# Tile 1's attention: the context rows' norm in nine steps, context projections in four parts, a modulation of three operations

## The chip, the core and the metric

The kernel runs on one core of a Trainium2 chip. The core has five engines that work side by side, each with its own instruction queue: TensorE (PE, matrix products; PEld are its weight loads), VectorE (DVE), ScalarE (ACT), GpSimd (POOL) and SyncE (SP), which here only issues DMA transfers. GpSimd's queue carries DMA issues too. An engine takes its instructions in order and waits on semaphores for what another engine or a DMA has to have done.

The metric is the device time of one execution in microseconds (us). The kernel before took 1836.33 us, the median of 3 runs (1835.45 to 1843.21).

## What is computed

A backbone of two layers over 1024 latent rows and 256 context rows of width 1024. Layer 0 is windowed attention with 16 heads of 64 (4 key-value heads, so 4 query heads to each), layer 1 a bidirectional state-space mixer (SSD). Ahead of each layer the rows are normed and modulated, behind it they are added through a gate:

```python
for i in range(DEPTH):
    shift, scale, gate = adaln(c, w_ada[i], b_ada[i])
    shift_c, scale_c, gate_c = adaln(c_ctx, w_ada[i], b_ada[i])
    u = rms_normalize(h) * (1.0 + scale[:, None]) + shift[:, None]
    uc = rms_normalize(hc) * (1.0 + scale_c) + shift_c
    ...
        y, yc = attention_mixer(u, uc, ...)   # layer 0
        y, yc = ssd_mixer(u, uc, ...)         # layer 1
    h = h + gate[:, None] * y
    if need_ctx_out:
        hc = hc + gate_c * yc
return rms_normalize(h) * final_norm_w
```

In the attention a block of 128 queries sees the key blocks beside it (up to 3) and the 2 blocks of context keys; context queries see only the context. The result is multiplied by silu(g) and goes through w_out, the output projection.

## The kernel before

The rows lie as columns: a row tile holds 128 features by n rows, and a full set of rows is 8 such pieces (k or m from 0 to 7). There are three row tiles: i = 0 and i = 1 are 512 latent rows each, i = 2 the 256 context rows. For accuracy every product of a projection is made of three: each operand is split into a high and a low part in float32r (uH and uL for the rows, wh and wl for the weights), and `mm3` (lines 236 to 238) multiplies high by high, high by low and low by high. A weight half is loaded by SP (line 229, into wr), cast on ScalarE (wh, line 222) and the rest taken off on GpSimd in this stage (wl, line 224).

Rows are normed by `rstd_c` (two small matmuls, line 367 with line 369's copy to sbuf as its end) and by `modulate` (line 290), which for one piece multiplies h by the row factor r (line 297, VectorE), applies scale and shift (line 298, ScalarE), casts to uH (line 299, ScalarE) and subtracts for uL (line 300, VectorE). It is called 40 times: for tile 1's and the context's rows of layer 0 by the first norm, and for all three tiles of layer 1.

The attention (`attention`, line 695) goes over units of one query block and one key-value head, 8 context units, then 16 of tile 0, then 16 of tile 1. `att_front` loads a unit's queries (qs and qz on GpSimd's DMA queue, sgt on SP's), makes the four heads' scores (lines 645 and 646), and the softmax (line 649 on VectorE, 651 on ScalarE). `att_back` then goes over the key blocks: four transposes (line 670), a cast to ph on ScalarE (674), a subtraction to pl on VectorE (675), and two matmuls with the values (676 and 677). qz holds one head's queries with zeros in the other half; the zeros are written once, by the memset of line 711, on VectorE.

After each key block `tick` advances the filler, so that TensorE has projections to do while the softmax runs. The filler is a list of generators; one call of `advance` runs one of them up to its next yield, a part. `tick` spreads the parts evenly: by the time of key block s of the stage's count, total x s / count parts are done. `self.tc.high_priority` and `issue_after` around them say where the scheduler may place the part: behind a matmul of the attention a few blocks back.

In tile 1's attention the filler is `out_steps(2)`, the context rows' output projections, and then `out_steps(0)`, tile 0's. `one(m)` makes one of 8 pieces of the output: it loads and splits the weights, loads the residual into the ring of two slots named h1 (SP), multiplies in PARTS = 8 parts (each one contraction step, three matmuls of n columns), adds through the gate (line 736, VectorE), stores h to DRAM (SP), squares it (ScalarE) and adds the squares up (line 744, GpSimd). `fin` norms the tile for layer 1: `rstd_c`, then for each of the 8 pieces a load of h from DRAM into the same ring of two (line 756) and `modulate`, all in one part. So the order of the filler's parts is: 64 for the context, 1 for its norm, 64 for tile 0, 1 for its norm: 130, which is what `total[1]` says. Its tile 1 counterpart, `out_steps(1)`, runs after the attention.

Line numbers are those of the kernel before.

Of the kernel before, what the change touches and what calls it, by code (L numbers as in the profile page):

```python
# [9 lines left out]
F32 = mybir.dt.float32  # L10
BF16 = mybir.dt.bfloat16
F32R = mybir.dt.float32r
AF = mybir.ActivationFunctionType
ALU = mybir.AluOpType
# [3 lines left out]
P = 128  # L18
D = 1024
KT = D // P  # L20
# [9 lines left out]
HD = 64  # L30
# [12 lines left out]
    pj=1, S=2, pt=2, pv=1,  # L43
# [5 lines left out]
AHEAD = 1  # L49
PACE = 4  # L50
PARTS = 8
SLACK = (0, 0, 0)
QC = 5
FIRST = 5
# [50 lines left out]
class Kernel:  # L105
# [13 lines left out]
    def t(self, pool, shape, dt, tag, bufs=None):  # L119
        self.n += 1  # L120
        kw = {"bufs": bufs or BUFS.get(tag, 1)}
        return pool.tile(shape, dt, tag=tag, name=f"{tag}_{self.n}", **kw)
# [167 lines left out]
    def modulate(self, layer, h, r, i, k):  # L290

        nc = self.nc
        c = 0 if i < 2 else 1
        m = self.mod[layer]
        sc, sh = m[:, 8 + k, c : c + 1], m[:, k, c : c + 1]
        uh, ul = self.uH[i][:, k, :], self.uL[i][:, k, :]
        nc.vector.tensor_mul(h, h, r)
        nc.scalar.activation(h, h, AF.Identity, bias=sh, scale=sc)
        nc.scalar.copy(uh, h)
        nc.vector.tensor_sub(ul, h, uh)  # L300


    def xin(self, i):
# [80 lines left out]
    def norm0(self, c0, p, wvp):  # L384
# [80 lines left out]
        for n in (0, 2):  # L465
            self.ada0(n, raws[n], ps)
        modulate(0)
        for x in range(G0 // 2):
            half(0, x)
# [22 lines left out]
        with last():  # L492
            self.load_rope(p, 0, LAT)
            load_nat(2)
            load_x(2)
        modulate(1)
        for x in range(G0):
            half(1, x)
# [196 lines left out]
    def attention(self, c0, ckv):  # L695
        nc, t, a = self.nc, self.t, self.a
        ps = self.psA
        BUFS.update(wr=2, wh=3, wl=3, sqt=2)
        self.wp = self.pool("wo", ctx=c0)
        self.pb = self.pool("back", ctx=c0)  # L700
        self.psm = self.pool("sm", ctx=c0)
        p = self.pool("att", ctx=c0)
        t(p, [P, 384], F32, "pad")
        cq = ExitStack()
        pq = self.pq = self.pool("qp1", ctx=cq)
        BUFS.update(qf=2, rope_b=1, qh=1, ql=1)
        self.load_rope(pq, 512, 512)
        oH, oL = [None] * 3, [None] * 3
        self.qz = [t(p, [P, R, P], F32R, f"qz{z}") for z in range(2)]
        for z in range(2):  # L710
            nc.vector.memset(self.qz[z][(1 - z) * HD : (2 - z) * HD].bitcast(F32), 0.0)

        def qg1(src, out, x):
            w = self.load_halves(a[src][x], nc.gpsimd)
            yield
            pj = []
            yield from self.proj_g(pj, ps, w, self.uH, self.uL, 1, parts=PARTS)
            out(pq, pj[0], x, 1)

        def out_steps(i):  # L720
            s, n = TT[i]
            c = 0 if i < 2 else 1
            st = {}

            def one(m):
                p = self.po
                w = self.load_halves(a["wo"][m], nc.gpsimd)
                yield
                h1 = t(self.o1, [P, n], F32, "h1k") if i == 1 else t(p, [P, n], F32, "h1")
                if i == 1:  # L730
                    st[m] = h1
                nc.sync.dma_start(h1, self.xin(i)[m * P : (m + 1) * P, :])
                out = []
                yield from self.proj_g(out, ps, w, oH, oL, i, "S" if i == 1 and m % 3 else "pj", parts=1 if i == 1 else PARTS)
                pj = out[0]
                nc.vector.scalar_tensor_tensor(h1, in0=pj[:, :n], scalar=self.mod[0][:, 16 + m, c : c + 1], in1=h1, op0=ALU.mult, op1=ALU.add)
                nc.sync.dma_start(self.h_d[m][i], h1)
                if m == 0:
                    st["acc"] = t(p, [P, n], F32, "sqa")
                    nc.scalar.activation(st["acc"], h1, AF.Square)  # L740
                else:
                    sq = t(p, [P, n], F32, "ut")
                    nc.scalar.activation(sq, h1, AF.Square)
                    (nc.vector if i == 1 else nc.gpsimd).tensor_tensor(st["acc"], st["acc"], sq, op=ALU.add)

            def fin():
                yield
                p = self.po
                r = self.rstd_c(p, st["acc"], n, D, rout=(p, [P, n], F32, "sqa"), dout=(p, [P, 512], F32, "dg0"))
                self.alloc_u(i)  # L750
                for k in range(KT):
                    if i == 1:
                        h = st[k]
                    else:
                        h = t(p, [P, n], F32, "h1")
                        nc.sync.dma_start(h, self.h_d[k][i])
                    self.modulate(1, h, r, i, k)

            return [lambda m=m: one(m) for m in range(KT)] + [fin]

        pr = [lambda x=x: qg1("wg", self.g_out, x) for x in range(8)] + [lambda x=x: qg1("wq", self.q_out, x) for x in range(8)]
        fill = {2: pr[:QC], 0: pr[QC:], 1: out_steps(2) + out_steps(0)}
        total = {2: QC * PARTS, 0: (16 - QC) * PARTS, 1: 16 * PARTS + 2}
        units = [(i, j, b) for i, blocks in ((2, range(8, 10)), (0, range(0, 4)), (1, range(4, 8))) for b in blocks for j in range(KV)]
        nkb = lambda b: 2 if b >= 8 else 2 + min(b + 2, 8) - max(b - 1, 0)
        count = {i: sum(nkb(u[2]) for u in units if u[0] == i) - SLACK[i] for i in range(3)}
        seen, done = [0, 0, 0], [0, 0, 0]
        self.last = []
        cur = nxt = None

        def tick(flush=False):

            seen[i] += 1
            while done[i] < (total[i] if flush else min(total[i], -(-total[i] * seen[i] // count[i]))):
                advance(i, self.last[max(-len(self.last), -PACE)])

        def advance(i, after):
            nonlocal cur, nxt
            with self.tc.high_priority(offset=-300), self.tc.issue_after(after):
                if cur is None:  # L780
                    cur = nxt or fill[i].pop(0)()
                    if nxt is None:
                        next(cur)
                    nxt = None
                    if fill[i]:
                        nxt = fill[i].pop(0)()
                        next(nxt)
                if next(cur, "end") == "end":
                    cur = None
            done[i] += 1  # L790

        pend = [self.att_front(p, x, *units[x]) for x in range(AHEAD)]
        for _ in range(FIRST):
            advance(2, self.scored.ins)
        for x, (i, j, b) in enumerate(units):
            if oH[i] is None:
                if i == 1:
                    i = 0
                    tick(True)
                    i = 1  # L800
                    cq.close()
                    self.po = self.pool("op", ctx=c0)
                n = TT[i][1]
                oH[i] = t(self.up, [P, KT, n], F32R, f"uH{i}")
                oL[i] = t(self.up, [P, KT, n], F32R, f"uL{i}")
            if x + AHEAD < len(units):
                pend.append(self.att_front(p, x + AHEAD, *units[x + AHEAD]))
            self.att_back(p, pend.pop(0), oH, oL, tick)
        tick(True)
        ckv.close()  # L810
        self.cf = ExitStack()
        self.pf = self.pool("front", ctx=self.cf, side="right")
        self.cdt = ExitStack()
        self.pdt = self.pool("dtp", ctx=self.cdt, side="right")
        with ExitStack() as c1:
            self.o1 = self.pool("o1", ctx=c1, side="right")
            steps = out_steps(1)
            for f in steps[:-1]:
                for _ in f():
                    pass  # L820
            self.dt_setup()
            for i, lo in ((2, 256), (0, 0)):
                n = TT[i][1] // 2
                self.dt_raw(self.dts[:, lo : lo + n], self.proj(ps, self.wdt, i), n)
            for _ in steps[-1]():
                pass
        BUFS.update(wr=2, wh=2, wl=2)
        if "u1" in self.dump:
            for i, (s, n) in enumerate(TT):
                self.dump_split("u1", self.uH[i], self.uL[i], i, n, s)  # L830
# [816 lines left out]
```

## Time and profile before

| what | value |
|---|---|
| median of 3 runs | 1836.33 us |
| the profiled execution, its time | 1840.92 us |
| the profiled execution, its span on the core | 1839.2 us |
| mean granted clock of TensorE | 0.988 of full |
| HBM traffic | 190.88 MB read, 35.13 MB written |

The span is the time from the first to the last instruction that the profiler saw; the time of the execution is a little longer. All times within the span are counted from its start, so "621.13" is a place. Tile 1's attention lies at about 500 to 690 us, the first norm and projections ahead of 100, and layer 1 from some 770 to the end. Busy times of engines overlap each other. Matmuls are pipelined and the rows of neighbours overlap (their ends are modelled); what a matmul costs in a dense stream is the distance between starts. In a row of waits stand the waiting engine with its tile and line, what it waited for, the total in us, how many times, and the longest; in a row of the timeline stand the start, the duration, the instruction, and in brackets the idle time ahead of it and what ended that.

### The profile page before, as it was taken

The page shows a single profiled execution, that of the slowest core. Times are in us where ns is not written, and L with a number is a line of the kernel's source. Part 1 is how long each engine was busy: PE and PEld are TensorE (multiplying, and loading weights), DVE is VectorE, ACT ScalarE, POOL GpSimd, SP SyncE. Part 2 cuts the span into 40 slices and gives each one's busy share as a digit, 9 for nine tenths or more (in the row PEclk, how much of TensorE's full clock was granted, in tenths as well). Part 3 has the DMA queues.
Part 4 walks back from the last instruction along what each step waited for, and adds up shares of the span by engine and source line. Part 5 has one row for each costly group of instructions (what it writes and reads, how often), then busy time and mean ns, then how long its engine had stood idle before and what let it go on. Part 6 is the DMA issues. An engine that isn't in the chain of part 4 may idle for free. (4 is left out here: it accounts for less than half of the span.)

```text
span 1839.2 us, 29059 instructions
## 1 busy us (share of the span) xinstructions
PE 1757.5 (96%) x10319; PEld 1503.1 (82%) x10319; DVE 1171.9 (64%) x2136; ACT 893.0 (49%) x1956; POOL 803.2 (44%) x1066
## 2 busy tenths in 40 slices
PE   6899999999999999899999999999999999999997
PEld 2697778888888787678889898988989898888886
DVE  4544426778887765674766757676675767675643
ACT  3722227777777765562443535344353434454422
POOL 1331116555566454102454554545455454554321
PEclk8999999999999999999999999999999999999998
DMA  8648855544455445321323323232232324456542
GB/s 303 241 127 263 284 179 141 121 97 107 112 130 130 109 129 187 99 70 41 87 69 78 93 66 83 76 92 67 80 93 64 86 73 101 148 165 171 180 138 69
DMA packets 212497, 227.62 MB, mean 124 GB/s; under 512 B 16384, under 2 KB 149632, under 8 KB 212352
## 3 DMA queue, kind: packets, MB, share of 16 engines
q1 hardware_dynamic: 178288, 207.12, 37.8%
q0 software_dynamic: 34064, 18.65, 5.6%
q8 instruction: 81, 1.33, 0.3%
q14 instruction: 64, 0.52, 0.1%
HBM read 190.88 MB, written 35.13 MB: 123 GB/s over the span
## 5 line engine op out<-in xcount | busy, mean ns | idle before, releaser
L236 PE MATMUL pj<-uH,wh 128*128 128x512 f32 (+1 forms) x712 | 256.4, 362 | 11.3 <-ACT uH L457 8.3
L238 PE MATMUL pj<-uH,wl 128*128 128x512 f32 (+1 forms) x712 | 243.7, 343 | 1.2 <-POOL wl L224 1.2
L237 PE MATMUL pj<-uL,wh 128*128 128x512 f32 (+1 forms) x712 | 244.2, 343 | 0.4 <-DVE uL L458 0.4
L1157 POOL TENSOR_TENSOR xw<-xn,dtdec 128x256 f32<-128x256 f32 x144 | 107.6, 750 | 199.5 <-PE psD L1182 127.1
L224 POOL TENSOR_TENSOR wl<-wr,wh 128x512 fp32r<-128x512 f32 x92 | 121.6, 1325 | 117.6 <-ACT wh L222 114.1
L1088 PE MATMUL pj<-uH,wh 128*128 128x512 f32 x512 | 165.9, 400 | 3.6 <-ACT bn L1042 2.2
L236 PEld LDWEIGHTS pj<-uH,wh 128*128 128x128 f32 x712 | 135.8, 191 | 39.2 <-ACT uH L457 9.6
L1088 PE MATMUL pj<-uL,wh 128*128 128x512 f32 x512 | 167.4, 400 | 0.2 <-DVE uL L300 0.2
L1088 PE MATMUL pj<-uH,wl 128*128 128x512 f32 x512 | 166.9, 400 | 0.7 <-DVE wl L1019 0.7
L1113 PE MATMUL pj<-wh,uH 128*128 128x256 f32 x512 | 151.7, 296 | 2.6 <-ACT xn L1042 2.6
L675 DVE TENSOR_TENSOR pl<-pt,ph 128x512 fp32r<-128x512 f32 x168 | 114.5, 687 | 58.2 <-ACT ph L674 57.0
L238 PEld LDWEIGHTS pj<-uH,wl 128*128 128x128 f32 x712 | 135.5, 190 | 18.4 <-POOL wl L224 2.1
L1113 PE MATMUL pj<-wh,uL 128*128 128x256 f32 x512 | 149.8, 293 | 0.0
L237 PEld LDWEIGHTS pj<-uL,wh 128*128 128x128 f32 x712 | 136.0, 191 | 16.9 <-issue 3.1
L1113 PE MATMUL pj<-wl,uH 128*128 128x256 f32 x512 | 147.1, 287 | 0.0
L222 ACT CAST wh<-wr 128x512 fp32r<-128x512 f32 (+1 forms) x132 | 84.7, 645 | 105.7 <-PE pj L237 82.2
L649 DVE CUSTOM_DVE_ANT_0 sm<-S,mask,nsink 128x640 f32<-128x640 f32 (+2 forms) x160 | 119.3, 771 | 22.0 <-PE S L646 14.7
L674 ACT CAST ph<-pt 128x512 fp32r<-128x512 f32 x168 | 97.6, 586 | 59.4 <-PE pt L670 55.6
L651 ACT ACTIVATE sm<-sm,nm 128x640 f32<-128x640 f32 (+2 forms) x160 | 118.7, 743 | 14.7 <-DVE nm L649 14.2
L1088 PEld LDWEIGHTS pj<-uH,wh 128*128 128x128 f32 x512 | 94.6, 189 | 23.8 <-ACT xn L1042 2.4
L1088 PEld LDWEIGHTS pj<-uL,wh 128*128 128x128 f32 x512 | 96.7, 189 | 20.6 <-DVE uL L300 0.5
L1088 PEld LDWEIGHTS pj<-uH,wl 128*128 128x128 f32 x512 | 96.4, 189 | 20.4 <-DVE wl L1019 1.1
(372 smaller groups left out, 4811.3 us busy)
## 6 DMA issues: line engine op xcount, KB each, us to landing
wr<-w_x SPq DMA_DIRECT2D x32, 512.0 KB, 3.9
M<-acs SPq DMA_DIRECT2D x64, 256.0 KB, 5.3
bw<-acs SPq DMA_DIRECT2D x64, 256.0 KB, 5.0
wr<-wo SPq DMA_DIRECT2D x48, 256.0 KB, 2.7
wr<-w_sk SPq DMA_DIRECT2D x24, 512.0 KB, 4.0
wr<-wg SPq DMA_DIRECT2D x40, 256.0 KB, 4.8
qs<-q POOLq DMA_DIRECT2D x40, 256.0 KB, 3.9
wada<-w_ada SPq DMA_DIRECT2D x16, 512.0 KB, 6.7
```

What stands on the lines that cost most here:

```text
L222: nc.scalar.copy(h, raw)
L224: (eng or nc.vector).tensor_tensor(l, raw, h, op=ALU.subtract)
L236: self.nc.tensor.matmul(ps, lh, rh, start=first and i == 0, stop=False)
L237: self.nc.tensor.matmul(ps, lh, rl, start=False, stop=False)
L238: self.nc.tensor.matmul(ps, ll, rh, start=False, stop=last and i == n - 1)
L649: nc.vector.tensor_tensor_reduce(out=sm[:, :W], in0=Sv, in1=self.mask[:, m0 : m0 + W], scale=-SCALE, scalar=self.nsink[:, 4 * j + r : 4 * ...
L651: nc.scalar.activation(sm[:, :W], sm[:, :W], AF.Exp, bias=nm[:, r : r + 1], scale=-1.0, accum_out=sums[:, r : r + 1])
L674: nc.scalar.copy(ph, ptf)
L675: nc.vector.tensor_sub(pl, ptf, ph)
L1088: nc.tensor.matmul(raw[:, 512 * i : 512 * i + 512], l[:, k, :], r[i][:, k, :], start=k + y == 0, stop=k == KT - 1 and y == 2)
L1113: nc.tensor.matmul(pj[:, c], l, r[:, k, :], start=c % 2 + q + k + y == 0, stop=c % 2 == 1 and q == 1 and k == 3 and y == 2)
L1157: nc.gpsimd.tensor_tensor(xw, X(st, c).rearrange("p (r h) -> p r h", r=R), self.dtdec[:, c, hd(d, g)].unsqueeze(2).broadcast_to([P, R, HP] ...
```

## The change

Four edits, all of which the diff shows:

1. `modulate` has three operations: h becomes h times scale times r (VectorE, one scalar_tensor_tensor), uH is h plus shift with the result in float32r (ScalarE), and uL is (h plus shift) minus uH (VectorE). In the values of h itself the shift is no longer included; h is not read afterwards.
2. The zeros of qz are written by GpSimd.
3. The context's output projections are made in CPARTS = 4 parts of six matmuls in place of 8 parts of three.
4. The context's norm is no longer a part of the filler. It is cut into nine steps, the row factor and eight modulations, held in `self.side`; `advance` runs the next one after every SIDE = 6 parts of tile 0's projections, outside `high_priority` and `issue_after`. Its row factor goes into a buffer named ut in place of sqa. `total[1]` becomes 8 x (4 + 8) + 1 = 97.

```diff
+CPARTS = 4
+SIDE = 6
...
-        nc.vector.tensor_mul(h, h, r)
-        nc.scalar.activation(h, h, AF.Identity, bias=sh, scale=sc)
-        nc.scalar.copy(uh, h)
-        nc.vector.tensor_sub(ul, h, uh)
+        nc.vector.scalar_tensor_tensor(h, in0=h, scalar=sc, in1=r, op0=ALU.mult, op1=ALU.mult)
+        nc.scalar.activation(uh, h, AF.Identity, bias=sh)
+        nc.vector.scalar_tensor_tensor(ul, in0=h, scalar=sh, in1=uh, op0=ALU.add, op1=ALU.subtract)
...
-            nc.vector.memset(self.qz[z][(1 - z) * HD : (2 - z) * HD].bitcast(F32), 0.0)
+            nc.gpsimd.memset(self.qz[z][(1 - z) * HD : (2 - z) * HD].bitcast(F32), 0.0)
...
-                yield from self.proj_g(out, ps, w, oH, oL, i, "S" if i == 1 and m % 3 else "pj", parts=1 if i == 1 else PARTS)
+                yield from self.proj_g(out, ps, w, oH, oL, i, "S" if i == 1 and m % 3 else "pj", parts={0: PARTS, 1: 1, 2: CPARTS}[i])
...
+            def norm():
+                p = self.po
+                rout = (p, [P, n], F32, "ut" if i == 2 else "sqa")
+                st["r"] = self.rstd_c(p, st["acc"], n, D, rout=rout, dout=(p, [P, 512], F32, "dg0"))
+                self.alloc_u(i)
+
+            def mod(k):
+                if i == 1:
+                    h = st[k]
+                else:
+                    h = t(self.po, [P, n], F32, "h1")
+                    nc.sync.dma_start(h, self.h_d[k][i])
+                self.modulate(1, h, st["r"], i, k)
+
             def fin():
                 yield
...
-            return [lambda m=m: one(m) for m in range(KT)] + [fin]
+                for f in steps:
+                    f()
+
+            steps = [norm] + [lambda k=k: mod(k) for k in range(KT)]
+            if i == 2:
+                self.side = steps
+            return [lambda m=m: one(m) for m in range(KT)] + ([] if i == 2 else [fin])
...
-        total = {2: QC * PARTS, 0: (16 - QC) * PARTS, 1: 16 * PARTS + 2}
+        total = {2: QC * PARTS, 0: (16 - QC) * PARTS, 1: KT * (CPARTS + PARTS) + 1}
...
             done[i] += 1
+            if i == 1 and self.side and done[i] > KT * CPARTS and (done[i] - KT * CPARTS) % SIDE == 0:
+                self.side.pop(0)()
```

More of the change, by code (lines that the diff above doesn't have):

```diff
@@ L744, in one @@
                     (nc.vector if i == 1 else nc.gpsimd).tensor_tensor(st["acc"], st["acc"], sq, op=ALU.add)
+            def norm():
[10 more added lines that the diff above has]
+                self.modulate(1, h, st["r"], i, k)
             def fin():
                 yield
[L748 to L757, printed above, removed]
-            return [lambda m=m: one(m) for m in range(KT)] + [fin]
+                for f in steps:
[4 more added lines that the diff above has]
+            return [lambda m=m: one(m) for m in range(KT)] + ([] if i == 2 else [fin])
         pr = [lambda x=x: qg1("wg", self.g_out, x) for x in range(8)] + [lambda x=x: qg1("wq", self.q_out, x) for x in range(8)]
         fill = {2: pr[:QC], 0: pr[QC:], 1: out_steps(2) + out_steps(0)}
-        total = {2: QC * PARTS, 0: (16 - QC) * PARTS, 1: 16 * PARTS + 2}
+        total = {2: QC * PARTS, 0: (16 - QC) * PARTS, 1: KT * (CPARTS + PARTS) + 1}
         units = [(i, j, b) for i, blocks in ((2, range(8, 10)), (0, range(0, 4)), (1, range(4, 8))) for b in blocks for j in range(KV)]
@@ L809, in attention @@
         tick(True)
+        assert not self.side
         ckv.close()
```

## The prediction

> **What bounds the kernel now.** I read the page first, then the waits of TensorE over the whole run, then windows over tile 1's attention, then the rows of single places.
>
> ```profile
> span 1839.2 us, 29059 instructions
> PE 1757.5 (96%) x10319; PEld 1503.1 (82%) x10319; DVE 1171.9 (64%) x2136; ACT 893.0 (49%) x1956; POOL 803.2 (44%) x1066
> ```
>
> TensorE is busy for 96% of the span, and the change leaves its 10,319 matmuls as they are. So work saved on ScalarE or VectorE is worth nothing by itself: only TensorE's idle time (1839.2 - 1757.5 = 81.7 us) can shrink, and the stretches in which its clock is lowered. The waits of PE on other engines, totals, times and longest, in the places that the change touches:
>
> ```profile
> PE pv L677 <- DVE pl L675: 7.6, 17, 1.7
> PE pj L236 <- DVE gq L553: 3.6, 1, 3.6
> PE S L646 <- DVE qz L711: 1.8, 1, 1.8
> PE pj L238 <- POOL wl L224: 1.2, 2, 1.0
> ```
>
> Three of them are single events. I take them in the order of size.
>
> **The burst of the context norm.** Tile 1's attention is some 76 key blocks (ticks) with filler between. Each tick advances 130/76 = 1.71 parts before: first 64 parts of 3 matmuls of 256 columns, then the norm of the context rows as one part, then 64 parts of 3 matmuls of 512 columns. Windows over it: length, busy time of PE, PEld, DVE, ACT and POOL (instructions), granted clock, DMA share, GB/s. The first window lies in the context projections, the second holds the norm, the third lies in tile 0's projections and runs into tile 1's.
>
> ```profile
> 505.00:595.00 90.00, 87.65 (x596) 78.02 (x595) 70.61 (x150) 69.97 (x155) 58.23 (x82) 1.00 0.54 134
> 595.00:628.00 33.00, 29.54 (x150) 22.53 (x150) 26.33 (x62) 26.20 (x62) 12.63 (x21) 0.95 0.34 87
> 628.00:716.00 88.00, 86.79 (x461) 71.05 (x459) 47.49 (x102) 50.82 (x111) 49.57 (x61) 1.00 0.46 138
> ```
>
> Busy time hides how well TensorE is packed, so I price the work by pitch. Key blocks are counted by the transposes (line 670, four to a block), here PE and PEld of that line alone for the same windows:
>
> ```profile
> 505.00:595.00 90.00, 23.99 (x162) 19.62 (x160) 1.00 0.54 134
> 595.00:628.00 33.00, 8.74 (x56) 7.16 (x56) 0.95 0.34 87
> 628.00:716.00 88.00, 14.20 (x96) 11.78 (x96) 1.00 0.46 138
> ```
>
> That is 40.5, 14 and 24 blocks. The filler's triples are counted by line 236, one of each three:
>
> ```profile
> 505.00:595.00 90.00, 22.59 (x69) 13.02 (x69) 1.00 0.54 134
> 595.00:628.00 33.00, 2.46 (x6) 0.94 (x5) 0.95 0.34 87
> 628.00:716.00 88.00, 30.72 (x75) 13.98 (x75) 1.00 0.46 138
> ```
>
> The starts of adjacent matmuls give the pitch, 0.23 us at 512 columns and 0.12 at 256:
>
> ```profile
> 695.63 0.39 PE L237 MATMUL pj<-uL,wh 128*128 128x512 f32 x1
> 695.86 0.40 PE L238 MATMUL pj<-uH,wl 128*128 128x512 f32 x1
> 510.16 0.28 PE L237 MATMUL pj<-uL,wh 128*128 128x256 f32 x1
> 510.28 0.28 PE L238 MATMUL pj<-uH,wl 128*128 128x256 f32 x1
> ```
>
> So a triple costs 0.69 or 0.36 us. A key block with its share of scores then costs (88 - 75 x 0.69)/24 = 1.51 us in the third window, and in the first, where by form 64 triples are of 256 columns and 5 of 512, (90 - 64 x 0.36 - 5 x 0.69)/40.5 = 1.57. I take 1.55. The burst's window should thus last 14 x 1.55 + 6 x 0.69 = 25.8 us, with 0.2 for the norm's own small matmuls 26.0. It lasts 33.0: **7.0 us are lost**. The timeline shows how:
>
> ```profile
> 621.13 0.43 DVE L297 TENSOR_TENSOR h<-h,sqa 128x256 f32<-128x256 f32 x1 [2.04 <-DMA h<-h]
> 621.48 0.68 DVE L675 TENSOR_TENSOR pl<-pt,ph 128x512 fp32r<-128x512 f32 x1
> 622.21 0.57 PE L677 MATMUL pv<-pl,v 128*128 128x512 f32 x1 [1.66 <-DVE pl L675]
> 622.50:625.90 3.40, 3.40 (x14) 2.94 (x14) 3.03 (x8) 3.01 (x8) 0.41 (x2) 0.50 0.00 0
> ```
>
> VectorE stands 2.04 us at the modulation's load of h, the pl of the next key block is queued behind it, TensorE stands 1.66 us for that pl, and the granted clock is 0.50 for the 3.40 us that follow (the last row is a window over them). TensorE has 14 blocks but only 6 triples of filler there: the norm's part and its neighbours fill a tick without a projection, so nothing covers the softmax chain.
>
> The Trainium skill (TensorE: Matmul & The Clock Gate, section "Part 1: The HAM clock gate") says that the gate halves the clock after a whole idle window of about 3.4 us. The trace differs: here a wait of 1.66 us was enough. By the rule the 3.4 us at half clock, worth 1.7, would belong to something else and could outlive the burst; the burst's term would be 5.3 in place of 7.0.
>
> The change cuts the fin of the context rows into nine steps (rstd, then eight modulations), one after every SIDE = 6 parts of tile 0's projection. Parts: 8 x 4 for the context, 8 x 8 + 1 for tile 0, 97 over 76 ticks = 1.28 a tick. The context takes 32/1.28 = 25 ticks (38 before), tile 0 51 (38 before); a tick carries 1.28 x 0.72 = 0.92 us of filler, then 1.28 x 0.69 = 0.88, where it carried 1.71 x 0.36 = 0.62 and 1.18. The built order bears this out: on VectorE tens of instructions lie between one step and the next, and the PE sequence holds the same 9,582 matmuls, filler between all key blocks. The work of a step (two VectorE operations of some 0.43, one on ScalarE of 0.60 or less) meets some 6/1.28 = 4.7 ticks of 1.55 + 0.88 = 2.43 us, that is 11 us of TensorE's work. Both SBUF engines have room: in the densest of the windows above VectorE is busy for 70.61 of 90.00. Term: **-7.0**, bounds -2 (each step still costs a little: 5 of the 7 come back over nine steps, 0.55 each) and -10 (the many small waits on pl, 7.6 less 1.66, shrink as well).
>
> What the side steps are queued with: each issues a load of h on SP's queue from the ring of 2 named h1, which tile 0's residuals share. A residual's load may have to wait until a modulation has read the slot, and a modulation's load until a residual's store is done; behind it on SP stand the loads of sgt and of the next weights. A weight pair is used every 51/8 = 6.4 ticks, 15 us, and a load lands quickly, so a blocked SP of a few us is covered; were that cover gone, the third rival below is the price.
>
> ```profile
> h<-h SPq DMA_DIRECT2D x16, 128.0 KB, 2.2
> wr<-wo SPq DMA_DIRECT2D x48, 256.0 KB, 2.7
> ```
>
> **The modulation in three operations.** By form, 512 columns (busy, mean ns, idle before); the last row is the nearest to the two new operations, a scalar_tensor_tensor with a scalar from memory:
>
> ```profile
> L297 DVE TENSOR_TENSOR h1k<-h1k,sqa 128x512 f32<-128x512 f32 x8 | 4.9, 686 | 0.1
> L298 ACT ACTIVATE h1k<-h1k,mod 128x512 f32<-128x512 f32 x8 | 6.3, 813 | 0.2 <-DVE h1k L297 0.2
> L299 ACT CAST uH<-h1k 128x512 fp32r<-128x512 f32 x8 | 4.7, 608 | 0.0
> L300 DVE TENSOR_TENSOR uL<-h1k,uH 128x512 fp32r<-128x512 f32 x8 | 5.2, 684 | 1.3 <-ACT uH L299 1.3
> L1413 DVE SCALAR_TENSOR_TENSOR uL<-uL,fw,y 128x512 f32<-128x512 f32 x4 | 2.7, 746 | 0.0
> ```
>
> ScalarE loses one operation in each of 40 modulations: 24 x 0.61 + 16 x 0.40 = 21 us, VectorE gains 80 x 0.06 = 5 us at most. The one ScalarE operation left has a float32r result and a bias, which no row shows: between 0.61 (the cast) and 0.81 (the activation). I take 0.75; the chain of one modulation gets 0.67 shorter, with ends of 0.8 and 0.55. Only where TensorE waits on that chain does it count.
>
> First, the start, where tile 1's and the context's rows are modulated while the first projections run:
>
> ```profile
> 84.66 2.96 DVE L300 TENSOR_TENSOR uL<-uL,uH 128x512 fp32r<-128x512 f32 x3
> 87.54 2.76 DVE L297 TENSOR_TENSOR xc<-xc,rr 128x256 f32<-128x256 f32 x8
> 90.22 0.68 DVE L300 TENSOR_TENSOR uL<-uL,uH 128x512 fp32r<-128x512 f32 x1
> 90.83 0.67 DVE L553 SCALAR_TENSOR_TENSOR gq<-gq,pj 128x512 f32<-128x512 f32 x1
> 91.55 0.58 PE L236 MATMUL pj<-wh,uH 128*128 128x256 f32 x1 [3.58 <-DVE gq L553]
> 90.00:96.80 6.80, 5.25 (x24) 5.25 (x25) 5.95 (x16) 5.27 (x15) 2.22 (x4) 0.50 0.26 56
> ```
>
> The gq for which TensorE waits 3.58 us stands behind 6.4 us of modulation on VectorE itself, which the change makes slightly longer (16 x 0.06 = 1.0). Against it, one L515 operation of 0.68 comes after gq in the new order, and VectorE waits less for ScalarE's casts (8 x 0.61 = 4.9 us less there). Afterwards TensorE is at half clock for 6.8 us, worth 3.4. The two nearly cancel: **-1**, bounds +2 and -5 (half of the clock's and half of the wait's 3.58 gone).
>
> Second, tile 0's fin after the attention. The new fin carries three operations; the stretch of 716 to 772 holds weight waits (the line 224 row above and its like for the next projection, 0.9) that ScalarE's queue feeds with its casts. **-1**, bounds 0 and -2.8, all of those waits. Third, tile 1's modulation at the start of layer 1, where its L300 waited 1.3 us for L299: **-0.5**, bounds +3 and -3, since the built order there moves instructions by up to some 23 places on VectorE and nothing shows which way that falls.
>
> **The memsets of qz** go from VectorE to GpSimd.
>
> ```profile
> 270.32 0.48 DVE L711 MEMSET qz<- 64x512 f32 x1 [0.16 <-issue]
> 270.86 0.50 PE L646 MATMUL S<-kL,qz 128*128 128x256 f32 x2 [1.82 <-DVE qz L711]
> 273.63 0.76 POOL L626 DMA_DIRECT2D qs<-q  x1 [13.50 <-PE S L646]
> ```
>
> TensorE waits 1.82 us for a memset that VectorE reaches only at 270.32. GpSimd idles there (13.50 us ahead of its next operation), so it can do it early. The first loads of qs and qz stand behind them on GpSimd's queue and land some 3.9 us after their issue by their DMA row; they were issued at 257, so a delay of some us still ends ahead of 270. What is late next is the memset's other reader, the score itself: **-1.2**, bounds 0 (the load of qz on the same tile is then the last) and -1.8.
>
> **The sum.** -7.0 - 1 - 1 - 0.5 - 1.2 = -10.7 us. The profiled execution took 1840.92 us, 1.7 more than its span; it lies 4.6 above the median 1836.33. So 1840.92 - 10.7 = 1830.2 in its terms, and 1836.33 - 10.7 = **1825.6 us** for the median; I say 1825.5.
>
> **The rivals.** About 0.5%, 9.2 us, is what a measurement of this kernel tells from no change: the bounds are 1827.1 and 1845.5.
>
> *The loss moves.* What the burst lost is lost again as ordinary pl waits: the context ticks are denser (0.92 us of filler in place of 0.62, and the weight splits on GpSimd, 1.3 us each, come in pairs every 25/8 x (1.55 + 0.92) = 7.7 us in place of every 38/8 x (1.55 + 0.62) = 10.3), so VectorE and GpSimd run closer to TensorE. For it: VectorE and ScalarE already run at 78% of the first window. Against: TensorE is at 87.65 of 90.00 there in spite of it. Price: the burst is worth -2 in place of -7, and the start, tile 0's fin and layer 1 give half of their 2.5: -4.5; 1832.
>
> *Slower: the ring of h1.* Each of the eight modulations waits on its load as the one at 621.13 did, because the load on SP stands behind a residual whose slot is not free. Then every step costs what that event did: 1.66 us of wait and half of 3.40 us of clock, 3.4 us; eight make 27, and from the fourth stall on the forecast gain is gone (3 x 3.4 = 10.2). With six of eight: 20.4 - 10.7 = +9.7, 1846; with all, 1853. For it: SP takes its instructions in order, and in the new order the loads of modulations and residuals alternate in two slots. Against: 11 us lie between steps, the load takes 2.2, and the filler of 0.88 us a tick now stands between the scores where the burst had none.
>
> *More than the sum.* The start loses its wait of 3.58 and a slice of 3.4 us at half clock (1.7), and the small pl waits shrink: -3 and -3 more; 1819.
>
> That the steps stay lumped, so that the change doesn't do what it says, is a rival that the built order excludes for TensorE and VectorE.
>
> **Chances.** Forecast 0.50, with its own range 1819.5 to 1830.5 from the bounds of the terms taken together; moved loss 0.23; slower 0.14; more 0.13. Under 1827.1 lie 0.37 of the forecast's 0.50 and all of the last: faster 0.50. Over 1845.5 lie 0.11 of the slower case: 0.11. Between: 0.39. The range 1817 to 1840 leaves out a third of the "more" case and most of the slower one, under 0.2.
>
> **What would show it.** Right: no window of 33 us in tile 1's attention that lasts over 2 us more than 1.55 a block, 0.69 or 0.36 a triple; no half clock in it; the wait on qz gone; L299's casts gone, with ScalarE's busy time down by some 16 to 21 us and TensorE's idle time by some 8. The wait on gq about as long as before. Wrong: rows of VectorE waiting on the DMA of h once a step, waits on pl that total as much as before, a weight load that lands after its cast is wanted, or half-clock stretches at new places.

## The result and the profile after

The changed kernel takes 1823.84 us, the median of 5 runs (1821.60 to 1825.46), against 1836.33 (1835.29 to 1844.62): the ratio is 0.9921, with a 95% interval of 0.9900 to 0.9941. The prediction said 1825.5, faster by more than 0.5%. The sum was near, but not each of its terms, as the stretches show.

The profiled execution took 1824.64 us. Its page:

```profile
span 1822.9 us, 28990 instructions
PE 1749.4 (96%) x10319; PEld 1501.8 (82%) x10319; DVE 1179.6 (65%) x2134; ACT 875.2 (48%) x1916; POOL 807.4 (44%) x1068
```

ScalarE has 40 instructions and 17.8 us less, the casts. TensorE's time outside its busy time fell from 81.7 to 73.5 us; the other half of the 16.3 us by which the span is shorter lies within "busy", in denser packing (the mean granted clock is not higher: 0.988 before, 0.987 after). So I read the change by stretches. All kernels here have 10,319 matmuls, and at the counts below the same matmul stands in each, or its neighbour in the pipeline; where the order differs, at most six of those ahead of count 4500 are others. A stretch is the time from the start of one to the start of the other, worked out from the traces; the first begins with the first matmul, some 11 us into the span, and the rest ends with the start of the last, some 8 us ahead of the span's end. 0 to 1350 holds the first norm and projections, 1350 to 1500 the memsets and the first scores, 1500 to 2700 the attention of the context and tile 0, 2700 to 3900 tile 1's attention with its filler, 3900 to 4500 tile 0's and tile 1's norms and layer 1's start, 4500 to 9900 the steady part of layer 1.

```
                              0-1350  1350-1500  1500-2700  2700-3900  3900-4500  4500-9900   rest
before                         249.3       31.0      214.0      210.7      137.3      915.4   62.2
after                          246.5       33.6      214.1      203.3      127.1      914.8   64.0
after, second profile          241.4       32.5      214.0      203.5      126.9      914.7   63.9
e1 modulation alone            245.4       33.4      214.0      214.5      129.3      914.6   64.0
e1, second profile             247.0       33.4      214.1      213.4      130.1      914.7   63.7
e2 steps and parts alone       245.8       33.2      214.0      205.1      137.7      915.4   63.8
e3 after, memset on VectorE    247.1       33.3      214.0      202.5      127.5      904.1   63.6
e4 after, context in 8 parts   242.2       32.5      214.2      204.9      128.8      914.8   63.6
e5 after, norm as one part     245.9       32.6      214.1      207.3      126.7      903.6   63.6
e7 memset alone                246.1       32.5      214.0      211.2      136.5      915.4   63.6
e8 after, 4 ops in tile 1      247.0       32.6      214.0      202.9      130.0      915.6   63.6
e9 after, step every part      247.1       32.5      214.0      204.0      125.1      914.8   62.2
e12 after, step every 4th      244.8       32.5      214.0      202.3      127.3      905.3   64.1
e13 the same, memset VectorE   245.7       31.0      214.0      202.7      126.2      914.8   63.6
```

The second profiles (after, e1) tell how far a figure can be trusted: tile 1's attention and what follows repeat within 1.1 us, the start does not (246.5 and 241.4 for one and the same program).

**The burst.** The stretch that lost 7.0 us, 595 to 628, in the windows of after, all engines:

```profile
595.00:628.00 33.00, 32.87 (x189) 27.86 (x188) 28.27 (x58) 24.91 (x55) 18.61 (x28) 1.00 0.44 118
```

The same window, transposes alone (four to a key block):

```profile
595.00:628.00 33.00, 7.95 (x56) 6.86 (x56) 1.00 0.44 118
```

And the first matmul of each triple alone:

```profile
595.00:628.00 33.00, 7.73 (x17) 3.22 (x18) 1.00 0.44 118
```

The 14 key blocks are as many as before, but with 17 triples in place of 6: by the prediction's prices 14 x 1.55 + 17 x 0.69 = 33.4 us of work in 33.0. Nothing is lost, and the granted clock stays at 1.00. The eight modulations are spread over 588 to 668 us, so this window holds only some of them; over 500 to 715 us TensorE's waits on pl are, first in before, then in after:

```profile
PE pv L677 <- DVE pl L675: 5.0, 11, 1.7
PE pv L678 <- DVE pl L676: 1.4, 6, 0.5
```

The granted clock over the whole stretch of tile 1's attention is 1.00 in after and 0.99 in before. VectorE still waits for the loads of h, in the waits of VectorE in tile 1's attention:

```profile
DVE h L299 <- DMA h<-h: 2.8, 4, 1.1
```

Four waits of 1.1 us at most: the ring of two did not become the bound.

**The memsets.** TensorE's wait on qz is gone. In its place, waits of TensorE over the run:

```profile
PE S L647 <- DVE nm L650: 3.2, 2, 1.8
```

and what VectorE and TensorE did there, then the window that follows:

```profile
267.31 0.48 DVE L650 CUSTOM_DVE_ANT_0 sm<-S,mask,nsink 128x256 f32<-128x256 f32 x1
269.62 0.48 DVE L650 CUSTOM_DVE_ANT_0 sm<-S,mask,nsink 128x256 f32<-128x256 f32 x1 [1.82 <-DMA sg<-qf]
270.17 0.58 PE L647 MATMUL S<-kHH,qs 128*128 128x256 f32 x1 [1.82 <-DVE nm L650]
270.50:275.90 5.40, 5.40 (x15) 4.24 (x15) 0.69 (x5) 1.75 (x8) 2.20 (x5) 0.50 0.39 73
```

The first score's maximum starts 4.1 us earlier than before (271.38 there; 2.8 of it come from the stretch ahead), but the second one writes a buffer that must wait for the DMA store of sg from qf, and TensorE stands as long as it did for the memset. Half clock follows.

**The start.** The wait on gq (3.6 us) has turned into three, 4.1 us together:

```profile
PE pj L238 <- DVE rope_b L514: 2.3, 1, 2.3
PE pj L238 <- DVE v L589: 1.6, 1, 1.6
PE pj L238 <- DVE gq L554: 0.2, 1, 0.2
```

**The modulation.** By form, tile 1's eight pieces in after:

```profile
L299 DVE SCALAR_TENSOR_TENSOR h1k<-h1k,mod,sqa 128x512 f32<-128x512 f32 x8 | 5.4, 746 | 0.1
L300 ACT ACTIVATE uH<-h1k,mod 128x512 fp32r<-128x512 f32 x8 | 5.3, 720 | 0.3 <-DVE h1k L299 0.3
L301 DVE SCALAR_TENSOR_TENSOR uL<-h1k,mod,uH 128x512 fp32r<-128x512 f32 x8 | 5.5, 745 | 0.0
```

The prices held: 0.72 us where 0.75 was said, and 0.746. What they are worth did not: the stretch around the norms of tiles 0 and 1, matmuls 3900 to 4500, is 10.2 us shorter. TensorE's waits in it (716.0 to 853.2), the largest of before:

```profile
PE pj L236 <- ACT dt L899: 2.8, 1, 2.8
PE pj L1088 <- ACT bn L1042: 2.2, 1, 2.2
PE psD L1078 <- ACT sqa L369: 1.7, 1, 1.7
```

and of after (708.5 to 835.6):

```profile
PE pj L1101 <- ACT wh L1028: 2.9, 1, 2.9
PE pj L1052 <- ACT xn L1055: 1.6, 1, 1.6
PE pj L238 <- ACT dt L912: 0.8, 1, 0.8
```

All rows of that view add up to 13.9 us before and 8.3 after. In the other kernels with four operations throughout (e7, e2) they make 14.5 and 14.4, in those with three 8.2 to 11.4. The wait on sqa is not part of the difference: e1 and e5 have it too, with 1.7 us. The wait on dt can be followed on ScalarE and TensorE, first in before:

```profile
757.13 1.04 ACT L1015 CAST wh<-wr 128x1024 fp32r<-128x1024 f32 x1 [2.19 <-DMA wr<-w_x]
758.09 1.47 ACT L899 ACTIVATE dt<-pj,db 32x128 f32<-32x128 f32 x4
759.61 0.80 PE L236 MATMUL pj<-uH,wdth 128*128 128x512 f32 x1 [2.83 <-ACT dt L899]
```

and the same three instructions of after:

```profile
745.00 1.04 ACT L1028 CAST wh<-wr 128x1024 fp32r<-128x1024 f32 x1
746.49 1.47 ACT L912 ACTIVATE dt<-pj,db 32x128 f32<-32x128 f32 x4 [0.45 <-PE pj L240]
748.02 0.50 PE L238 MATMUL pj<-uH,wdth 128*128 128x512 f32 x1 [0.78 <-ACT dt L912]
```

Before, the cast of layer 1's first weight waits 2.19 us for its load, with the eviction of dt queued behind it; after, the load was issued earlier (740.98 on SP's queue, where before it stood until 752.68 behind stores of h1k) and the cast waits for nothing. Then the 45 us from tile 1's modulation on, first before, then after:

```profile
769.00:814.00 45.00, 40.22 (x214) 33.48 (x215) 37.99 (x64) 34.11 (x66) 1.04 (x1) 1.00 0.28 66
```

```profile
755.00:800.00 45.00, 42.08 (x203) 34.84 (x203) 38.98 (x63) 29.17 (x57) 1.94 (x1) 0.92 0.25 54
```

VectorE is busy for 84% and ScalarE for 76% of the first. In these 45 us themselves no gain shows: TensorE runs 203 matmuls in place of 214, though some are longer. After has a wait of 2.9 us there that before has not, on a weight's cast, with half clock behind (granted 0.62 from 770 to 779, which costs 9 x 0.38 = 3.4 us). The wait on bn, which ends at 813.69 in before, is gone. In matmuls 3900 to 4500 of before, half clock follows in three places, together 5.1 us by the same working. So in this pair of profiles 5.6 of the 10.2 us are waits, 1.7 the clock, and some 3 denser packing. The split is not firm: in the second profile of after the waits make 8.8 us and the granted clock is 0.99 in place of 0.97, and the stretch takes 126.9 us all the same.

What ScalarE does ahead of that bn shows that the casts of the norm do not hold it up directly. In before the last of these casts ends at 782.3 us, and ScalarE has idle times behind it, the last one of 3.40 us up to 807.95. Then come operations on M, a weight's cast, hf and pj, all of other work in layer 1, and only then bn, at 813.06. In after the same copy of bn stands ahead of all of these and starts at 792.32. That is another order, made by the scheduler, the program that sets the order of instructions. TensorE's order differs too: from matmul 4168 on, the kernels with three operations for tile 1 leave the order that before, e2, e7 and e8 share.

### The profile page after: what moved, and what is told of

Same layout as the page of the kernel before. It is cut to its first block, busy times and chain, and to the rows that moved or that the text cites. A ratio compares the mean times of both kernels' runs of the same rounds, so it can differ in the third digit from the quotient of the medians.

```text
span 1822.9 us, 28990 instructions
## 1 busy us (share of the span) xinstructions
PE 1749.4 (96%) x10319; PEld 1501.8 (82%) x10319; DVE 1179.6 (65%) x2134; ACT 875.2 (48%) x1916; POOL 807.4 (44%) x1068
## 5 line engine op out<-in xcount | busy, mean ns | idle before, releaser
L1170 POOL TENSOR_TENSOR xw<-xn,dtdec 128x256 f32<-128x256 f32 x144 | 103.6, 722 | 190.2 <-PE psD L1195 113.0
L239 PEld LDWEIGHTS pj<-uL,wh 128*128 128x128 f32 x712 | 137.3, 193 | 16.7 <-issue 3.0
```

The lines of the kernel that those rows point to most:

```text
L239: self.nc.tensor.matmul(ps, lh, rl, start=False, stop=False)
L1170: nc.gpsimd.tensor_tensor(xw, X(st, c).rearrange("p (r h) -> p r h", r=R), self.dtdec[:, c, hd(d, g)].unsqueeze(2).broadcast_to([P, R, HP] ...
```

## The experiments

**e1, the modulation alone.** The kernel before with:

```diff
-        nc.vector.tensor_mul(h, h, r)
-        nc.scalar.activation(h, h, AF.Identity, bias=sh, scale=sc)
-        nc.scalar.copy(uh, h)
-        nc.vector.tensor_sub(ul, h, uh)
+        nc.vector.scalar_tensor_tensor(h, in0=h, scalar=sc, in1=r, op0=ALU.mult, op1=ALU.mult)
+        nc.scalar.activation(uh, h, AF.Identity, bias=sh)
+        nc.vector.scalar_tensor_tensor(ul, in0=h, scalar=sh, in1=uh, op0=ALU.add, op1=ALU.subtract)
```

> The kernel before with the modulation of three operations alone. In the traces of before and after, the same matmul starts 2.8 us earlier at 258 us, 7.4 earlier at 716, 9.2 earlier at 754 and 18.2 earlier once layer 1 runs evenly. Theory A: the gain at the start (2.8) and that of layer 1's start (9) both come from the shorter modulation, so this kernel takes about 11 us less than before, some 1825, and the burst in tile 1's attention stays, shorter by at most 2. Theory B: layer 1's gain comes from the attention being left in another state (loads and stores on SP's queue, the scheduler's order), so this kernel gains only 2 to 4, some 1833.

Measured: 0.9972 (0.9953 to 0.9992), 1837.15 us beside 1840.47. By place both theories were half right: 3900 to 4500 took 129.3 in place of 137.3 without any step in the attention, so that gain is the modulation's. The total hides it, because tile 1's attention became 3.8 slower.

A second profile asked whether that was chance:

> A second profile of the first experiment (the modulation of three operations alone). In the first, tile 1's attention took 214.5 us, 3.8 more than before, and 10.7 us were lost in the burst. If a burst of the shorter modulation is slower by itself, 213 to 216 again; if that was the throttle's place in one execution, 209 to 212. The stretch after the attention, matmuls 3900 to 4500, at 126 to 130 either way.

213.4: it was not. This kernel's attention is 2.7 to 3.8 us slower than that of before. In the first profile 595 to 640 us hold 14 blocks and 18 triples, 34.3 us of work with the norm's 0.2, and 10.7 are lost, in before 17 and 17, 38.3, and 6.7. Why stays open: the order of TensorE's matmuls 3300 to 3900 differs from that of before too, and no run took the operations apart.

**e2, the steps and the four parts alone.** The changed kernel with e1's edit undone and the memsets on VectorE.

> The changed kernel with the modulation of four operations and the memsets on VectorE, so the nine steps and the four parts alone. Theory A: it gains what tile 1's attention shows, some 7 us, and nothing at the start or in layer 1: about 1829. Theory B: it gains that and layer 1's 9 as well: about 1820. If the side steps are worth nothing without the shorter modulation: 1836.

0.9967 (0.9949 to 0.9986). Theory A: attention 205.1 (5.6 gained), nothing after it (137.7).

**e3, the memsets back.**

```diff
-            nc.gpsimd.memset(self.qz[z][(1 - z) * HD : (2 - z) * HD].bitcast(F32), 0.0)
+            nc.vector.memset(self.qz[z][(1 - z) * HD : (2 - z) * HD].bitcast(F32), 0.0)
```

> The changed kernel with the memsets of qz back on VectorE. Theory A: in the changed kernel the second score's maximum on VectorE waited 1.82 us for the DMA store of sg, which ends at an absolute place, so the memset would have been hidden by that wait; putting it back costs nothing, 1822 to 1826, and tile 0's attention starts at the same place within 0.5. Rival, by the prediction's term: 1.2 us slower, the wait of TensorE on the memset of 1.8 is back. Third: the half clock that followed at 270.5 to 275.9 goes, and it is some 2 us faster.

0.9839 (0.9808 to 0.9871), 1810.39 us: some 14 faster than the changed kernel, which none of the three foresaw. At the memsets there is no difference (33.3 and 33.6). The gain lies over 500 us later, in layer 1's steady part, 904.1 in place of 914.8. The scheduler had reached another order for layer 1, of which no line is edited: TensorE's order differs from that of after from matmul 4454 to 9720. Windows of all engines, after and then e3:

```profile
1100.00:1600.00 500.00, 491.05 (x3050) 437.91 (x3049) 346.46 (x577) 217.75 (x502) 253.79 (x348) 1.00 0.33 89
```

```profile
1100.00:1600.00 500.00, 495.59 (x3094) 444.09 (x3093) 349.18 (x598) 228.15 (x514) 265.85 (x355) 1.00 0.36 95
```

Waits of TensorE from 1150 to 1600 us, the largest of after, then of e3:

```profile
PE psX L1253 <- POOL xw L1170: 3.8, 4, 1.0
```

```profile
PE psX L1246 <- DVE y L1289: 2.6, 4, 0.6
```

44 more matmuls in 500 us, and a wait of 1.0 us per round that became one of 0.6. A round of 650 matmuls takes 107.05 us in the one order and 104.97 in the other. All waits of those 450 us add up to 6.8 and 3.8 us, some 0.7 a round; the rest of the 2.1 us stands in no wait.

**e5, the norm as one part.** The changed kernel with `fin` in the filler again for the context:

```diff
-            if i == 2:
-                self.side = steps
-            return [lambda m=m: one(m) for m in range(KT)] + ([] if i == 2 else [fin])
+            self.side = []
+            return [lambda m=m: one(m) for m in range(KT)] + [fin]
...
-        total = {2: QC * PARTS, 0: (16 - QC) * PARTS, 1: KT * (CPARTS + PARTS) + 1}
+        total = {2: QC * PARTS, 0: (16 - QC) * PARTS, 1: KT * (CPARTS + PARTS) + 2}
```

> The changed kernel with the context's norm as one part of the filler again (context projections still in four parts, modulation of three operations). Theory A: the burst's stall comes back at 2 to 6 us (the three operations make it shorter than the 7 of before), about 1829; windows without projections show a wait on pl or on the load of h. Rival: the denser filler and the shorter modulation had removed the stall by themselves, and the steps are worth nothing: 1824.

0.9868 (0.9837 to 0.9899), faster than the changed kernel, but only by layer 1's other order (903.6). At its own place the burst is back: attention 207.3, 4.0 more than after. Waits of TensorE at it, 560 to 640:

```profile
PE pv L678 <- DVE pl L676: 3.2, 4, 1.3
```

and a window over part of it, all engines, with the clock down again:

```profile
575.00:584.00 9.00, 7.33 (x35) 5.70 (x34) 7.00 (x12) 4.72 (x10) 3.21 (x4) 0.81 0.48 117
```

**e4, the context in eight parts** (CPARTS = 8).

> The changed kernel with the context's projections in eight parts again. Its order in layer 1 is that of the changed kernel, so the total compares. Theory A: the even filler (0.92 and 0.88 us a tick in place of 0.62 and 1.18) is worth part of the attention's gain: from the end of tile 0's attention to the end of tile 1's projections it lies between before (210.7 us) and after (203.3), at some 206, and the total is 2 to 4 slower than the changed kernel's 0.992 of before, ratio about 0.994. Rival: only the steps matter, 203 there and 0.992.

0.9912 (0.9886 to 0.9939): the total can't tell it from the changed kernel. The attention took 204.9, 1.6 more, which is little above the 1.1 within which a stretch repeats. VectorE waited more for h than in any other run:

```profile
DVE h L299 <- DMA h<-h: 8.0, 7, 1.7
```

**e7, the memsets alone.** The kernel before with the memset line of the change.

> The kernel before with the memsets of qz on GpSimd alone. Its order in layer 1 is that of before. Theory A: the 1.8 us wait on the memset is replaced by the wait of the second score's maximum on the store of sg, the stretch of 260 to 291 us gets no shorter than in before or in the first experiment (31.0 to 33.4, according to the granted clock), and the total stays within 0.2% of before. Rival, the prediction's term: 1.2 us faster; no more than that either, so the stretch and its waits decide and not the total.

0.9994 (0.9978 to 1.0010), the stretch 32.5 us, and in place of the wait on qz:

```profile
PE S L646 <- DVE nm L649: 3.2, 2, 1.8
```

**e8, four operations for tile 1 only.** The changed kernel with, at the head of `modulate`'s operations:

```diff
+        if layer == 1 and i == 1:
+            nc.vector.tensor_mul(h, h, r)
+            nc.scalar.activation(h, h, AF.Identity, bias=sh, scale=sc)
+            nc.scalar.copy(uh, h)
+            nc.vector.tensor_sub(ul, h, uh)
+            return
```

> The changed kernel with the modulation of four operations for tile 1 at the start of layer 1 alone (eight of the forty). Its built order in layer 1 is then that of before again. Theory A: the gain of layer 1's first 80 us (matmuls 4300 to 4500 took 43.0 us before, 35.7 after) is lost again, 41 to 44, and that of the stretch ahead of it (tile 0's norm, 94.3 before, 91.4 after) is kept: total 5 to 8 slower than the changed kernel, ratio 0.995 to 0.997. Theory B: the gain there comes from the stretch ahead arriving in another state; then 36 to 38 and 0.992.

0.9911 (0.9891 to 0.9932): the total did not move as expected. By place, matmuls 4300 to 4500 took 42.1, as before (43.0), which is theory A. After's 35.7 for them compares less well: in its order seventeen of the first 4300 matmuls are others, most of them longer. Matmuls 3900 to 4500 together compare cleanly: 130.0, 2.9 more than after and 7.3 less than before. In e8 TensorE has the order of before all through this stretch, so the 7.3 come without a new order: they belong to the shorter norm of tile 0 ahead of it, since e2 shows that the steps and parts give nothing there. The smaller part, 2.9, comes with tile 1's own modulation and with the other order of layer 1's start at once, and no run separates these two. The wait on bn, in before 2.19 us up to 813.69, is back in it:

```profile
799.38 0.73 PE L1107 MATMUL pj<-uH,wh 128*128 128x512 f32 x2 [2.74 <-ACT bn L1061]
```

**e9, a step after every part** (SIDE = 1).

> The changed kernel with the nine steps after consecutive parts of tile 0's projection (one every part in place of every sixth), so within some 7 ticks. Theory A: what counts is that a step has filler beside it; nine steps in 7 ticks load VectorE with some 0.9 x 1.3 us a tick more and wait for loads of 2.2 us each through two slots, so part of the stall is back: 1 to 4 us slower than the changed kernel, ratio 0.993 to 0.995, attention 204 to 207. Rival: the spacing does not matter once the steps are outside the filler's parts: 203 and 0.992. Slower rival of the prediction: every step waits on its load with half clock behind it: over 210 and over 0.996.

0.9915 (0.9886 to 0.9944), attention 204.0: 0.7 more than with six. That the steps stand beside filler counts, how far apart they are hardly. (In e5 the norm is not only one part, but also placed under the filler's `high_priority` and `issue_after`; which of the two makes its burst no run separates.)

**e12 and e13, a step after every fourth part** (SIDE = 4), e13 with the memsets on VectorE. Each reaches the other of layer 1's orders, the reverse of e3.

> The changed kernel with a step after every fourth part in place of every sixth, memsets on GpSimd as in the changed kernel. The built order of layer 1 is, for this value, the other one: that of the third experiment (memset on VectorE) and the fourth (burst), in which matmuls 6000 to 9900 took 663.6 and 663.2 us in place of 674.1. Theory C: the order of layer 1 that the scheduler happens to reach is worth 11 us whatever edit leads to it, so this kernel takes 663 to 664 there and is 9 to 13 faster than the changed kernel: ratio 0.984 to 0.987, attention 202 to 205 as with six. Rival: the gain of the third experiment came from the memset or from where its buffers lie, and this one has 674 and 0.992.

> The same with the memsets on VectorE. Its built order of layer 1 is that of the changed kernel. Theory C: 674 us for matmuls 6000 to 9900 and a ratio of 0.990 to 0.993, the reverse of what the memset's place did in the third experiment; at the memsets themselves no difference (the stretch at 260 to 291 within 0.8 of 33). Rival, the memset on VectorE is worth 11 by itself: 0.980 to 0.987.

0.9846 (0.9826 to 0.9865) and 0.9910 (0.9885 to 0.9935): theory C in both, 905.3 and 914.8 us. With 1810 us, e12 and e3 are the fastest kernels here.

Last, a second profile of the changed kernel, in the table above:

> A second profile of the changed kernel, to see how far a stretch repeats: tile 1's attention 203 within 1, matmuls 3900 to 4500 at 125 to 129, 4500 to 9900 at 915 within 0.5, the start (matmuls 0 to 1350) anywhere from 242 to 250, as the other kernels show.

1818.35 us: 203.5, 126.9 and 914.7 as expected, and a start of 241.4, just below what was said.

## Why the prediction was right, and where it was not

*The burst, -7.0: right.* 210.7 and 211.2 (before, e7) became 203.3 and 203.5. Taking one edit out of the changed kernel at a time costs 4.0 for the steps (e5), 1.6 for the four parts (e4) and 1.8 for the modulation (e2; 2.6 beside e3, which has its memsets on VectorE as e2 has). Each is from one profile, and figures under 2 are little above the 1.1 of a repeat. The prediction gave it all to the steps. Nor do the edits simply add up, since the modulation alone made it worse (e1). The 11 us of cover for a step were more than it needed (e9).

*Slower, the ring of h1: it did not come.* Even 8.0 us of waits on h in seven pieces (e4) left the attention at 204.9. The prediction's price of 3.4 us a stall came from a stall without filler beside it.

*The start, -1: not decided.* 249.3 in the profile of before is the longest of the fourteen; kernels with four operations show 245.8 to 249.3, those with three 241.4 to 247.1, and one program differs by 5.1 from itself. So the 2.8 us that after seems to gain there are not shown to be the change's. Before's profile lies 4.6 us over the median of its five runs, so any place counted from its start may carry as much.

*Tile 0's norm and layer 1's start, -1 and -0.5: the terms that were mis-sized.* Together they measure -10.2 (137.3 to 127.1; e1 alone -8.0 and -7.2), outside their bounds of -5.8. By e8 some 7.3 of it are tile 0's norm, put at -1 with a bound of -2.8, and 2.9 tile 1's, put at -0.5 with a bound of -3. The step that failed is "Only where TensorE waits on that chain does it count", read as VectorE's wait on line 299, 1.3 us, and TensorE's on the weights. The runs show in its place: in e8, where of these two norms only tile 0's is shorter, TensorE's wait on dt, which is other work of ScalarE, goes from 2.8 to 0.8 us, and all waits from 13.9 to 10.2. e1 shows that the operations do it and e2 that the steps do not. How much of it goes over ScalarE's queue and how much over SP's earlier load no run separates. The wait on bn goes with the order that the scheduler chose for layer 1's start, which the prediction named as the reason for its bounds there.

*The memsets, -1.2: wrong.* Nothing, by the stretch (31.0 to 33.4 on VectorE, 32.5 to 33.6 on GpSimd) and by the wait that takes the memset's place; e7's total (0.9994) fits, but its interval is too wide to tell 1.2 us from none. The prediction asked what is late next and named the score, or the load of qz; it was a buffer of the softmax that waits on a store. Its bound of 0 held.

*The sum.* -7.0 was right, -1.2 came to nothing, and -1.5 should have been -10. By place the attention gives 7.4, what follows 10.2 and the steady part 0.6, and the rest after matmul 9900 takes back 1.8: some 16 us without the start and the memsets' stretch, which vary. The ratio's interval allows 11 to 18, and the medians lie 12.5 apart. That the forecast came within 1.7 us of the median is in part luck: one term was short by 8.7 us, one was worth nothing, and the median of before from which it was counted, 1836.33 of five runs, lies below the 1840.47 and 1839.98 that 19 and 13 runs gave beside the experiments.

*What was not foreseen:* a rival in which an edit turns layer 1's order. The built order showed the last third unchanged, and TensorE's order in the traces is that of before from matmul 6903 on; in the first part of layer 1 it is not. Three of the kernels with small edits fell into a third order, worth 9.5 to 11 us in the steady part, as much as the whole forecast.

## What to carry to other kernels

Cut work that stops a filler into steps beside the filler; their spacing matters little once TensorE has something to do. Price a saved operation by the stretch it lies in: here waits on other work of the same engine shrank too, so look at all waits on that engine, and ask whether the saved operation also lets the scheduler choose another order. Where a scheduler orders the program, compare edits by stretches between the same matmuls, since a total of 1% can be an order that flipped far from the edit.

## What the runs showed of the hardware

VectorE's operations with both inputs in sbuf can be held while GpSimd runs a tensor operation. In after, on VectorE and then on GpSimd:

```profile
639.96 1.83 DVE L301 SCALAR_TENSOR_TENSOR uL<-h,mod,uH 128x256 fp32r<-128x256 f32 x1
641.71 0.68 DVE L676 TENSOR_TENSOR pl<-pt,ph 128x512 fp32r<-128x512 f32 x1
```

```profile
640.20 1.29 POOL L226 TENSOR_TENSOR wl<-wr,wh 128x512 fp32r<-128x512 f32 x1
```

The same operation takes 0.48 us elsewhere; here 1.83, about its own time and GpSimd's 1.29. The Trainium skill (SBUF — State Buffer, section "Who interferes with whom") says that these two engines share a pair of ports under an exclusive lock; the trace agrees. Of the sixteen operations of the context's steps five took 0.98 to 1.83 us, each beside a tensor operation of GpSimd; all sixteen took 12.1 us of VectorE in place of the 7.7 that 0.48 each would make. The attention was shorter all the same.

The clock again fell without a long idle stretch: in the memsets' stretch after two waits of 1.34 and 1.82 us with 0.5 us of matmuls between, for 5.4 us. The length of one wait does not decide it: the burst's wait of 1.66 us in before was followed by half clock, the wait of 1.74 us on sqa, which ends at 769.37 in the same profile, was not (granted 1.00 from 766 to 776).
